# Half of the residual's transposition by a trip through HBM, and the stores of the squared tiles on GpSimd's queue

## The chip, the cores and the metric

The kernel runs on one core of a Trainium2 chip. The metric is device time of one execution in microseconds (us). Five engines work side by side, each in the order of its own program: PE (matrix products), DVE (VectorE), ACT (ScalarE), POOL (GpSimd) and SP. SP, ACT and POOL also issue DMA transfers.

## The reference

The reference computes one decoder layer on 256 tokens of width 2048 in fp32: two kinds of attention behind one input projection, an output projection, and a squared-ReLU MLP of width 8192. What this case touches is the line between attention and MLP:

```python
x   = x + RMSNorm_post(concat_heads(A, B) @ W_out)
x   = x + RMSNorm_post2(W_down relu(RMSNorm_pre2(x) @ W_up)^2)
```

## The kernel before

**Products.** Every fp32 operand is split into two rounded parts, hi by ACT (line 314, or 318 with a gain) and lo by DVE (line 315, or 319 with a gain). A block is the sum of three matrix products on PE: hi·hi, lo·hi and hi·lo, each 128x128 by 128x512, one every 0.227 us when nothing stalls (line 304).

**Stages.** Input projection, attention, output projection (accumulators acc_o), the residual with its norm, the up-projection (acc_u), its evacuation (ReLU and square), the down-projection (y), the last norm. b is one of the two halves of 128 tokens.

**The residual.** A generator `residual(b)` (949 to 983) makes x in four parts of 512 columns (line 958, DVE). Sixteen tiles of 128x128 of x are turned on PE (line 308, tile ht, four tiles to a group), each group is split to hT_hi (ACT) and hT_lo (DVE), the left operand of the up-projection. POOL stores x (xkeep, line 974); ACT squares x for the norm (junkx).

**The up-projection** has eight chunks j of 1024 columns. Chunk 0 takes sixteen k-steps (one per 128 rows of W_up), with a weight tile raw loaded by SP and split. Chunks 1 to 7 begin with k-steps 6 to 10, then alternate: step w0, k 11 and 12, w1, k 13, w2, k 14 and 15. A "w" step replaces two k-steps by seven products instead of eight (`seven`, 351 to 389). Its pair of weight tiles, 1 MB, is one load into one of two buffers, ab and ab2 (line 379, from POOL; (j,1) below means step w1 of chunk j). From that pair DVE makes sums, t (366) and u (370, 371), and ACT and DVE split the pair's part, u and t. Two w steps of chunk 6 and 7 (last one, last two) are loaded by SP tile by tile instead. The left operands' sums are made in `left_sums` (1137 to 1168).

**Evacuation.** After a chunk's last product DVE adds the seven products' part to the four accumulators (line 1259), then four emptyings follow, (b,n) = (0,0), (0,1), (1,0), (1,1): ACT does ReLU (1043) and square (1044) to a tile r, ACT's queue stores it (rkeep, 1046), and `turn_u` later loads it back in another layout (1059) and turns it on DVE (1061). The names rkeep2_1, r2_1 and so on are column block and b: chunk j has column blocks 2j and 2j+1.

**What sets the order.** The program order of each engine is written out by a small planner, `Flow`: a modelled clock and a list of generators with due times; each `yield x` puts the generator x us later on that clock, and `pump` runs those that are due between PE's products. Weight tiles are planned in one list; a w step's load (`fetch`) and its sums are emitted two tiles ahead of its first tile, at the same place. So the order in which POOL meets a load and a store is fixed here, while each engine runs as fast as its operands come:

```python
SUMS_AHEAD = 2
at = max(len(weights.specs) - SUMS_AHEAD, after)
for n, f in (*more, (0, fetch), (-late_sums, sums), *((0, f) for f in last)):
evac.append(flow.start(up_evac(2 * j + n, b, accs[b, n], o + 0.6)))
yield UP_STEP * order
```

Of the kernel before, what the change touches and what calls it, by code (L numbers as in the profile page):

```python
# [18 lines left out]
F32 = mybir.dt.float32  # L19
# [3 lines left out]
AF = mybir.ActivationFunctionType  # L23
# [15 lines left out]
FF = 4 * D  # L39
# [6 lines left out]
CW = 1024  # L46
# [45 lines left out]
D_PAIR, D_KR = 3.5, 6.0  # L92
D_LOADED, D_LATENT, D_KV = (13.0, 9.0), 3.0, (1.0, 5.0, 7.0)
D_X0, D_X, D_SS, D_TAB = 8.0, 3.0, 3.0, (14.0, 20.0)
D_NORM, D_HT, D_SECOND = 4.5, 1.5, 4.0

UP_STEP = 2.4

D_BACK, D_TURN, D_NEG, D_LO, D_ADD = 12.0, 8.0, 9.0, 2.0, 26.0

# [171 lines left out]
def layer(nc, tc, io):  # L272
# [652 lines left out]
    def powers():  # L925
# [18 lines left out]
        for b in range(NB):  # L944
            for c in (slice(0, CW), slice(CW, D)):
                nc.vector.tensor_scalar_mul(xs[b][:, c], xs[b][:, c], pw[:, b:b + 1])
                yield 1.5

    def residual(b):

        po, yg, hT = late["po"], late["yg"], late["hT"]
        nc.vector.reduce_sum(ssr[b][:, 0:1], ssy[b], axis=mybir.AxisListType.X)
        r = rstd_of(ssr[b][:, 0:1], 1, D, f"post{b}", (pws[:, 0, b:b + 1], pws[:, 1, b:b + 1]))

        def update(ns):
            cs = [slice(n * 512, (n + 1) * 512) for n in ns]
            for c in cs:
                nc.vector.scalar_tensor_tensor(out=xs[b][:, c], in0=yg[b][:, c], scalar=r, in1=xs[b][:, c],
                                               op0=OP.mult, op1=OP.add)

        update((0, 1))
        yield D_NORM
        for n in range(4):
            t = tp_bank(f"ht{n}{b}")
            for k in range(4):
                transpose(t[:, k * P:(k + 1) * P], xs[b][:, n * 512 + k * P:n * 512 + (k + 1) * P])
            tv = t.rearrange("p (k s) -> p k s", k=4)
            if n in (0, 1):
                update((n + 2,))
            split(hT[0][:, 4 * n:4 * n + 4, b * P:(b + 1) * P], hT[1][:, 4 * n:4 * n + 4, b * P:(b + 1) * P], tv)  # L970
            parts[b] += 1
            yield D_HT
        for q in range(4):
            nc.gpsimd.dma_start(out=xkeep[b][32 * q:32 * q + 32], in_=xs[b][q::4, :])
        for n in range(4):
            c = slice(n * 512, (n + 1) * 512)
            junk = po.tile([P, 512], BF16, tag="junk", bufs=1, name=f"junkx{n}{b}")
            nc.scalar.activation(junk, xs[b][:, c], AF.Square, accum_out=ssx[b][:, n:n + 1])
            yield 0.5
# [9 lines left out]
    def h_done(k, b):  # L989
        flow.until(lambda: 4 * parts[b] > k)  # L990

    res = [None] * NB
    for ns in ((0, 1), (2,), (3,)):
        if len(ns) == 2:
            order = [(c, t, b) for ts in (range(4), range(4, 6), range(6, 8)) for c in range(2) for t in ts for b in range(NB)]
        else:
            order = [(0, t, b) for t, b in in_order(8, (0, APART[0] if ns == (3,) else 0))]
        for c, b, acc in proj(mixT, [ch_o[n] for n in ns], f"o{ns[0]}", order, heads_done):
            n = ns[c]
            if not late:  # L1000
                flow.finish(*workers)
                pb.release()
                lat.release()
                hp = pool("hp", "left")
                late["hT"] = [hp.tile([P, KD, S], F32R, name=f"hT_{w}") for w in ("hi", "lo")]
                po = late["po"] = pool("po", "right")
                late["g_post"] = po.tile([P, D], F32, name="g_post")
                nc.sync.dma_start(out=late["g_post"],
                                  in_=io["norm_attn_post"].partition_broadcast(P).rearrange("p o d -> p (o d)"))
                late["yg"] = [po.tile([P, D], F32, name=f"yg{b}") for b in range(NB)]  # L1010
                for b_ in range(NB):
                    xs.append(po.tile([P, D], F32, name=f"x{b_}"))
                    nc.sync.dma_start(out=xs[b_], in_=io["x"][b_ * P:(b_ + 1) * P, :])
                pw_chain = flow.start(powers())
            out_evac(n, b, acc[0])
            if n == 3:
                flow.finish(pw_chain)
                weights.ahead = AHEAD_NORM
                res[b] = flow.start(residual(b), b * D_SECOND)
                flow.pump()  # L1020
    hT = late["hT"]

# [13 lines left out]
    def up_evac(j, b, acc, order):  # L1036
# [4 lines left out]
        else:  # L1041
# [1 line left out]
        nc.scalar.activation(r, acc, AF.Relu, scale=rstd2[b])  # L1043
        nc.scalar.activation(r, r, AF.Square)
        keep = dram.tile([P, 512], F32, name=f"rkeep{j}_{b}")
        nc.scalar.dma_start(out=keep.rearrange("(a t) (q c) -> (t q) a c", a=4, q=4),
                            in_=r.rearrange("m (a c) -> m a c", a=4))
        flow.start(turn_u(j, b, keep), D_BACK + (8.0 if (j, b) == (GT - 1, NB - 1) else 0.0))

# [87 lines left out]
    def left_sums(kp):  # L1137
# [4 lines left out]
        hs = [t[:, k:k + 2, :].rearrange("p k s -> p (k s)") for t in hT]  # L1142
        tt(out=f, in0=hs[0].bitcast(F32), in1=hs[1].bitcast(F32), op=OP.add)
        for i in range(2):
            nc.vector.tensor_scalar_mul(f[:, i * S:(i + 1) * S], f[:, i * S:(i + 1) * S], gcol[:, 8 + k + i:9 + k + i])
        fs, qs = [x.rearrange("p (k s) -> p k s", s=P) for x in (f, q)]
        keep = kp >= min(N_SEVEN[1:])
        n = 512 if keep else 384
# [51 lines left out]
    def closing():  # L1200
        return [late["c"][:, i * 512:(i + 1) * 512] for i in range(4)]

    PARTS = ((0, 0), (0, 1), (1, 0), (1, 1))
    evac = []
    for j in range(FF // CW):
# [4 lines left out]
        else:  # L1210
            accs = {bn: bank(i, f"acc_u{j}_{bn[0]}{bn[1]}") for bn, i in at.items()}
        steps = wide_u[j]
        order = in_order(len(steps), (APART[1], 0)) if j == 0 else [(t, b) for t, (w, _, _) in enumerate(steps)
                                                                    for b in range(NB if w == "k" else 1)]
        for t, b in order:
            what, k, tiles = steps[t]
            if (j, t, b) == (0, 8, 0):
                flow.finish(*res)
                late["po"].release()
                mix.release()  # L1220
                late["up"] = pool("up", "right")
# [34 lines left out]
        if j:  # L1256

            for bn in PARTS:
                nc.vector.tensor_tensor(out=accs[bn], in0=accs[bn], in1=more[bn], op=OP.add)
# [177 lines left out]
def arrays_of(inputs):  # L1437
# [3 lines left out]
    a["x"] = np.ascontiguousarray(a["x"][order])  # L1441
    a["xt"] = np.ascontiguousarray(np.concatenate([a["x"], inputs["norm_attn_pre"]]).T)
    a["pos"] = np.ascontiguousarray(inputs["positions"].reshape(S)[order].reshape(NB, P).T)
    a["gains"] = np.ascontiguousarray(np.concatenate(
        [inputs[n].reshape(-1, P) for n in ("q_latent_norm", "kv_latent_norm", "norm_mlp_pre")]).T)
    a["w_down"] = np.ascontiguousarray(
        a["w_down"].reshape(FF // 512, 4, 4, 32, D).transpose(0, 2, 1, 3, 4).reshape(FF, D))
    q = a["w_uq"].reshape(QR, HB, NOPE + RB)
    kv = a["w_ukv"].reshape(KVR, HB, NOPE + 128)
    a["w_uq"] = np.ascontiguousarray(np.concatenate([x.reshape(QR, -1) for x in (q[:, :, :NOPE], q[:, :, NOPE:])], axis=1))  # L1450
    a["w_ukv"] = np.ascontiguousarray(np.concatenate([x.reshape(KVR, -1) for x in (kv[:, :, :NOPE], kv[:, :, NOPE:])], axis=1))
    for n in ("norm_attn_post", "norm_mlp_post"):
        a[n] = np.ascontiguousarray(inputs[n])
    a["consts"] = shape_constants(order)
# [21 lines left out]
```

## Time and profile before

| what | us |
|---|---|
| median of the three runs shown (1020.38 to 1021.37) | 1020.69 |
| profiled execution | 1022.37 |
| its span, first to last instruction | 1020.6 |
| PE busy in the span | 1009.9 |
| DVE busy | 841.5 |
| ACT busy | 624.8 |
| POOL busy | 101.3 |

The profile page counts busy time per engine, cuts the span into 40 slices, follows back the chain of work that ended last, and groups instructions by line. All times of single instructions are counted from the span's start. A row of a timeline gives start, duration, engine, line, operation, tiles, and in brackets the idle time ahead of it with what ended it. A row of the windows table gives the window, then for PE, the weight loads, DVE, ACT and POOL the busy us and the count, the granted clock, the busy share of the DMA engines and GB/s.

### The profile page before, as it was taken

The page shows a single profiled execution, that of the slowest core. Times are in us where ns is not written, and L with a number is a line of the kernel's source. Part 1 is how long each engine was busy: PE and PEld are TensorE (multiplying, and loading weights), DVE is VectorE, ACT ScalarE, POOL GpSimd, SP SyncE. Part 2 cuts the span into 40 slices and gives each one's busy share as a digit, 9 for nine tenths or more (in the row PEclk, how much of TensorE's full clock was granted, in tenths as well). Part 3 has the DMA queues.
Part 4 walks back from the last instruction along what each step waited for, and adds up shares of the span by engine and source line. Part 5 has one row for each costly group of instructions (what it writes and reads, how often), then busy time and mean ns, then how long its engine had stood idle before and what let it go on. Part 6 is the DMA issues. An engine that isn't in the chain of part 4 may idle for free.

```text
span 1020.6 us, 13297 instructions
## 1 busy us (share of the span) xinstructions
PE 1009.9 (99%) x4670; PEld 842.0 (83%) x4670; DVE 841.5 (82%) x1127; ACT 624.8 (61%) x824; POOL 101.3 (10%) x160
## 2 busy tenths in 40 slices
PE   9999999999999999999999999999999999999996
PEld 6888889898888788888888888888878888888885
DVE  6676747676656779998999989897999999898985
ACT  6585446555463567676666775676666665767661
POOL 0020302102101200000010100000110000211100
PEclk9999999999999999999999999999999999999999
DMA  8977759656687478778988979679989867888952
GB/s 286 367 248 269 244 167 310 220 173 194 199 320 209 174 286 260 245 258 247 293 271 279 284 215 302 190 255 339 346 271 389 292 241 257 296 305 327 368 188 82
DMA packets 109170, 267.07 MB, mean 262 GB/s; under 512 B 9520, under 2 KB 28464, under 8 KB 108464
## 3 DMA queue, kind: packets, MB, share of 16 engines
q1 hardware_dynamic: 65584, 175.14, 50.2%
q0 software_dynamic: 20144, 71.31, 21.1%
q10 hardware_dynamic: 23376, 19.78, 6.2%
q8 instruction: 36, 0.59, 0.2%
q14 instruction: 30, 0.25, 0.1%
HBM read 232.64 MB, written 33.56 MB: 261 GB/s over the span
## 4 chain that ended last, share of the span: by engine, by line
PE 89%; DVE 5%; DMA 2%; issue 2%; ACT 1%; POOL 0%; ACTq 0%; DVEq 0%; POOLq 0%; SPq 0%
PE acc_u L304 26%; PE y L304 19%; PE acc_o L304 8%; PE m L304 6%; PE acc_v L304 5%; PE md L304 5%; PE acc_qk L304 4%; PE acc_q L304 3%; PE acc_k L304 3%; PE acc_ckv L304 3%; DVE lo L315 2%; PE acc_cq L304 2%; DMA rkeep<-uT 1%; PE sc_b L304 1%; DMA raw<-in_w_in 1%
## 5 line engine op out<-in xcount | busy, mean ns | idle before, releaser
L315 DVE TENSOR_TENSOR lo<-raw,hi 128x1024 fp32r<-128x1024 f32 (+2 forms) x205 | 233.4, 1157 | 66.6 <-ACT hi L314 65.4
L314 ACT ACTIVATE hi<-raw 128x1024 fp32r<-128x1024 f32 (+2 forms) x205 | 202.5, 1005 | 75.5 <-DMA raw<-in_w_in 22.8
L304 PE MATMUL acc_u<-hi,hT_lo 128*128 128x512 f32 x386 | 150.3, 389 | 0.5 <-DVE hT_lo L315 0.5
L304 PE MATMUL acc_u<-hi,hT_hi 128*128 128x512 f32 x386 | 150.7, 390 | 0.0
L304 PE MATMUL acc_u<-lo,hT_hi 128*128 128x512 f32 x386 | 150.2, 389 | 0.0
L304 PE MATMUL y<-lo,uhi 128*128 128x512 f32 x358 | 139.4, 389 | 0.4 <-DVE lo L315 0.4
L304 PE MATMUL y<-hi,ulo 128*128 128x512 f32 x358 | 139.4, 389 | 0.1
L304 PE MATMUL y<-hi,uhi 128*128 128x512 f32 x358 | 139.3, 389 | 0.0
L318 ACT ACTIVATE hi<-raw,gcol 128x1024 fp32r<-128x1024 f32 x86 | 96.7, 1148 | 34.2 <-DMA raw<-in_w_up 13.7
L319 DVE SCALAR_TENSOR_TENSOR lo<-raw,gcol,hi 128x1024 fp32r<-128x1024 f32 x86 | 106.6, 1274 | 9.7 <-ACT hi L318 9.6
L304 PEld LDWEIGHTS acc_u<-hi,hT_lo 128*128 128x128 f32 x386 | 72.4, 188 | 16.0 <-DVE hT_lo L315 0.9
L304 PEld LDWEIGHTS acc_u<-hi,hT_hi 128*128 128x128 f32 x386 | 72.5, 188 | 14.9
L304 PEld LDWEIGHTS acc_u<-lo,hT_hi 128*128 128x128 f32 x386 | 72.5, 188 | 14.8
L304 PEld LDWEIGHTS y<-lo,uhi 128*128 128x128 f32 x358 | 67.2, 188 | 14.7 <-DVE lo L315 0.8
L304 PEld LDWEIGHTS y<-hi,ulo 128*128 128x128 f32 x358 | 67.2, 188 | 14.4 <-DVE ulo L315 0.5
L304 PEld LDWEIGHTS y<-hi,uhi 128*128 128x128 f32 x358 | 67.2, 188 | 14.0
L315 DVE TENSOR_TENSOR lo<-st_down,hi 128x1024 fp32r<-128x1024 f32 x46 | 55.0, 1219 | 0.8 <-ACT hi L314 0.8
L304 PE MATMUL acc_o<-hi,mixT_hi 128*128 128x512 f32 x128 | 51.3, 401 | 0.0
L314 ACT ACTIVATE hi<-u 128x1024 fp32r<-128x1024 f32 (+1 forms) x33 | 32.3, 980 | 30.3 <-PE y L304 12.0
L304 PE MATMUL md<-hi,s 128*128 128x512 f32 x138 | 49.9, 389 | 0.0
L304 PE MATMUL acc_o<-hi,mixT_lo 128*128 128x512 f32 x128 | 49.9, 390 | 0.0
L304 PE MATMUL acc_o<-lo,mixT_hi 128*128 128x512 f32 x128 | 49.8, 389 | 0.0
(356 smaller groups left out, 2046.4 us busy)
## 6 DMA issues: line engine op xcount, KB each, us to landing
raw<-in_w_up SPq DMA_DIRECT2D x86, 512.0 KB, 4.9
raw<-in_w_down SPq DMA_DIRECT2D x82, 512.0 KB, 6.3
raw<-in_w_in SPq DMA_DIRECT2D x55, 512.0 KB, 5.6
ab<-in_w_up POOLq DMA_DIRECT2D x17, 1024.0 KB, 6.9
raw<-in_w_out SPq DMA_DIRECT2D x32, 512.0 KB, 4.6
ab_down<-in_w_down POOLq DMA_DIRECT2D x11, 1024.0 KB, 9.3
ulo<-ukeep POOLq DMA_DIRECT2D x20, 512.0 KB, 6.3
rkeep<-r ACTq DMA_DIRECT2D x28, 256.0 KB, 3.6
```

The source lines that it names most:

```text
L304: nc.tensor.matmul(out, a, b, start=start, stop=stop)
L314: nc.scalar.activation(hi, src, AF.Copy)
L315: nc.vector.tensor_tensor(out=lo, in0=src, in1=hi.bitcast(F32), op=OP.subtract)
L318: nc.scalar.activation(hi, src, AF.Copy, scale=g)
L319: nc.vector.scalar_tensor_tensor(out=lo, in0=src, scalar=g, in1=hi.bitcast(F32), op0=OP.mult, op1=OP.subtract)
```

## The change

Five things change.

1. Of each b, the upper half of x (columns 1024 to 2047) is no longer turned on PE. `trip` stores it to HBM (keeph, 512 KB, POOL), `turn_h` loads it back into yg (POOL), DVE turns it in two instructions of 128x512, and ACT and DVE split it from there. Sixteen of the 32 ht transposes go. Rows of W_up and their gains are permuted on the host to fit.
2. In chunk 0 the tiles of b=1 run two behind those of b=0 after the first seven tiles of both.
3. rkeep is stored from POOL's queue, not ACT's.
4. The third and fourth emptying of a chunk are due 1.9 and 1.4 us later on the planner's clock ((3.4 − 2.6) and (4.2 − 3.6), times UP_STEP 2.4).
5. In `left_sums` two multiplies by a gain move from DVE to ACT, and due times of the residual's steps are set anew.

On POOL, behind the residual, the queue of the kernel before holds the w steps' loads, one after the other (ab and ab2 are the two buffers, ukeep a store of transposed squares much later; rstd_pre2 is the norm's factor):

```order
L506 TENSOR_TENSOR rstd_pre21_3394<-t_pre21_3393,neg_half_85 128x1
L379 DMA ab2_3458<-in_w_up 128x2x1024
L379 DMA ab_3457<-in_w_up 128x2x1024
L379 DMA ab2_3458<-in_w_up 128x2x1024
L379 DMA ab_3457<-in_w_up 128x2x1024
L379 DMA ab2_3458<-in_w_up 128x2x1024
```

These are (1,1), (1,2), (2,0), (2,1) and (2,2); (1,0) is issued by SP. The same stretch with the change, to the load of (3,0):

```order
L507 TENSOR_TENSOR rstd_pre21_3468<-t_pre21_3467,neg_half_85 128x1
L1077 DMA rkeep0_0_3595<-r0_0_3592 128x4x128
L1077 DMA rkeep1_0_3614<-r1_0_3611 128x4x128
L1077 DMA rkeep0_1_3668<-r0_1_3665 128x4x128
L1077 DMA rkeep1_1_3691<-r1_1_3688 128x4x128
L380 DMA ab2_3478<-in_w_up 128x2x1024
L380 DMA ab_3477<-in_w_up 128x2x1024
L380 DMA ab2_3478<-in_w_up 128x2x1024
L1077 DMA rkeep2_0_4000<-r2_0_3997 128x4x128
L1077 DMA rkeep3_0_4023<-r3_0_4020 128x4x128
L1077 DMA rkeep2_1_4057<-r2_1_4054 128x4x128
L380 DMA ab_3477<-in_w_up 128x2x1024
```

The four stores of chunk 0 now stand ahead of (1,1), and of chunk 1's stores three stand ahead of (2,1); in each later chunk up to the sixth it is the same three. On ACT, at the end of chunk 1, before (u and t of step (2,0), hi166 is the hi part for k = 11 of chunk 2):

```order
L314 ACTIVATE hi164_4038<-u2_0_4013 128x1024
L1043 ACTIVATE r2_1_4051<-acc_u1_10_3645,rstd_pre21_3394 128x512
L1044 ACTIVATE r2_1_4051<-r2_1_4051 128x512
L1046 DMA rkeep2_1_4054<-r2_1_4051 128x4x128
L314 ACTIVATE hi165_4059<-t2_0_4012 128x1024
L1043 ACTIVATE r3_1_4072<-acc_u1_11_3646,rstd_pre21_3394 128x512
L1044 ACTIVATE r3_1_4072<-r3_1_4072 128x512
L1046 DMA rkeep3_1_4075<-r3_1_4072 128x4x128
L318 ACTIVATE hi166_4088<-raw166_4086,gcol_69 128x1024
```

and after:

```order
L315 ACTIVATE hi164_4028<-u2_0_4003 128x1024
L315 ACTIVATE hi165_4044<-t2_0_4002 128x1024
L1074 ACTIVATE r2_1_4054<-acc_u1_10_3633,rstd_pre21_3468 128x512
L1075 ACTIVATE r2_1_4054<-r2_1_4054 128x512
L319 ACTIVATE hi166_4073<-raw166_4071,gcol_69 128x1024
L1074 ACTIVATE r3_1_4080<-acc_u1_11_3634,rstd_pre21_3468 128x512
L1075 ACTIVATE r3_1_4080<-r3_1_4080 128x512
```

The third square, r2_1, moved behind the split of t, the fourth behind hi166, and the stores are gone from ACT. On DVE the same stretch, after, has the order that it had before:

```order
L316 TENSOR_TENSOR lo165_4045<-t2_0_4002,hi165_4044 128x1024
L367 TENSOR_TENSOR t2_1_4066<-ab_3477 128x1024
L371 TENSOR_TENSOR u2_1_4067<-t2_1_4066,ab_3477 128x512
L372 TENSOR_TENSOR u2_1_4067<-u2_1_4067,ab_3477 128x512
L320 SCALAR_TENSOR_TENSOR lo166_4074<-raw166_4071,gcol_69,hi166_4073 128x1024
```

The first reader of (2,1), t2_1, still follows lo165, the lo part of t2_0, directly. SP's queue is the same in both; on PE only the sixteen transposes are gone.

The diff, the host's part cut to its core:

```diff
--- before.py
+++ after.py
@@ -92,9 +92,10 @@
 D_PAIR, D_KR = 3.5, 6.0
 D_LOADED, D_LATENT, D_KV = (13.0, 9.0), 3.0, (1.0, 5.0, 7.0)
 D_X0, D_X, D_SS, D_TAB = 8.0, 3.0, 3.0, (14.0, 20.0)
-D_NORM, D_HT, D_SECOND = 4.5, 1.5, 4.0
-
-UP_STEP = 2.4
+D_NORM, D_HT, D_SECOND = (4.5, 4.8), (1.5, 2.5), 2.5
+D_AWAY, D_HERE, D_GROUP, D_SQUARE, D_KEEP = (9.0, 3.0), (6.8, 8.0), (1.2, 0.1), (4.0, 5.5, 8.5), 3.5
+UP_STEP, EVAC = 2.4, (0.6, 1.6, 3.4, 4.2)
 
 D_BACK, D_TURN, D_NEG, D_LO, D_ADD = 12.0, 8.0, 9.0, 2.0, 26.0
 
@@ -946,6 +947,22 @@
                 nc.vector.tensor_scalar_mul(xs[b][:, c], xs[b][:, c], pw[:, b:b + 1])
                 yield 1.5
 
+    def turn_h(b, keep):
+        back, turned = [late["yg"][b][:, i * CW:(i + 1) * CW] for i in range(2)]
+        nc.gpsimd.dma_start(out=back.rearrange("p (n f) -> p n f", n=2), in_=keep.rearrange("(n p) f -> p n f", p=P))
+        yield D_HERE[b]
+        hT = late["hT"]
+        tv = [turned[:, i * 512:(i + 1) * 512].rearrange("p (k s) -> p k s", k=4) for i in range(2)]
+        for i in range(2):
+            nc.vector.transpose(tv[i].rearrange("p k (t q) -> p k q t", q=4),
+                                back[:, i * 512:(i + 1) * 512].rearrange("p (q k c) -> p k q c", q=4, k=4))
+            yield D_GROUP[b]
+        for i in range(2):
+            split(*[x[:, 8 + 4 * i:12 + 4 * i, b * P:(b + 1) * P] for x in hT], tv[i])
+            parts[b] += 1
+            yield 0.3
     def residual(b):
 
         po, yg, hT = late["po"], late["yg"], late["hT"]
@@ -958,25 +975,39 @@
                 nc.vector.scalar_tensor_tensor(out=xs[b][:, c], in0=yg[b][:, c], scalar=r, in1=xs[b][:, c],
                                                op0=OP.mult, op1=OP.add)
 
+        def trip():
+            update((2, 3))
+            keep = dram.tile([2 * P, 512], F32, name=f"keeph{b}")
+            nc.gpsimd.dma_start(out=keep.rearrange("(g t) (q c) -> (t q) g c", g=8, q=4),
+                                in_=xs[b][:, CW:].rearrange("m (g c) -> m g c", g=8))
+            res.append(flow.start(turn_h(b, keep), D_AWAY[b]))
         update((0, 1))
-        yield D_NORM
-        for n in range(4):
+        if not b:
+            trip()
+        yield D_NORM[b]
+        for n in range(2):
             t = tp_bank(f"ht{n}{b}")
             for k in range(4):
                 transpose(t[:, k * P:(k + 1) * P], xs[b][:, n * 512 + k * P:n * 512 + (k + 1) * P])
             tv = t.rearrange("p (k s) -> p k s", k=4)
-            if n in (0, 1):
-                update((n + 2,))
             split(hT[0][:, 4 * n:4 * n + 4, b * P:(b + 1) * P], hT[1][:, 4 * n:4 * n + 4, b * P:(b + 1) * P], tv)
             parts[b] += 1
-            yield D_HT
+            if b and not n:
+                trip()
+            yield D_HT[b]
+        if b:
+            yield D_KEEP
         for q in range(4):
             nc.gpsimd.dma_start(out=xkeep[b][32 * q:32 * q + 32], in_=xs[b][q::4, :])
+        yield D_SQUARE[2 * b]
         for n in range(4):
             c = slice(n * 512, (n + 1) * 512)
             junk = po.tile([P, 512], BF16, tag="junk", bufs=1, name=f"junkx{n}{b}")
             nc.scalar.activation(junk, xs[b][:, c], AF.Square, accum_out=ssx[b][:, n:n + 1])
             yield 0.5
+        if not b:
+            yield D_SQUARE[1]
         nc.vector.reduce_sum(ssr[b][:, 1:2], ssx[b], axis=mybir.AxisListType.X)
         rstd2[b] = rstd_of(ssr[b][:, 1:2], 1, D, f"pre2{b}", (1.0 / D, pws[:, 2, b:b + 1]))
         if b == NB - 1:
@@ -989,7 +1020,7 @@
     def h_done(k, b):
         flow.until(lambda: 4 * parts[b] > k)
 
-    res = [None] * NB
+    main, res = [None] * NB, []
     for ns in ((0, 1), (2,), (3,)):
         if len(ns) == 2:
             order = [(c, t, b) for ts in (range(4), range(4, 6), range(6, 8)) for c in range(2) for t in ts for b in range(NB)]
@@ -1016,7 +1047,7 @@
             if n == 3:
                 flow.finish(pw_chain)
                 weights.ahead = AHEAD_NORM
-                res[b] = flow.start(residual(b), b * D_SECOND)
+                main[b] = flow.start(residual(b), b * D_SECOND)
                 flow.pump()
     hT = late["hT"]
 
@@ -1043,7 +1074,7 @@
         nc.scalar.activation(r, acc, AF.Relu, scale=rstd2[b])
         nc.scalar.activation(r, r, AF.Square)
         keep = dram.tile([P, 512], F32, name=f"rkeep{j}_{b}")
-        nc.scalar.dma_start(out=keep.rearrange("(a t) (q c) -> (t q) a c", a=4, q=4),
+        nc.gpsimd.dma_start(out=keep.rearrange("(a t) (q c) -> (t q) a c", a=4, q=4),
                             in_=r.rearrange("m (a c) -> m a c", a=4))
         flow.start(turn_u(j, b, keep), D_BACK + (8.0 if (j, b) == (GT - 1, NB - 1) else 0.0))
 
@@ -1142,7 +1173,8 @@
         hs = [t[:, k:k + 2, :].rearrange("p k s -> p (k s)") for t in hT]
         tt(out=f, in0=hs[0].bitcast(F32), in1=hs[1].bitcast(F32), op=OP.add)
         for i in range(2):
-            nc.vector.tensor_scalar_mul(f[:, i * S:(i + 1) * S], f[:, i * S:(i + 1) * S], gcol[:, 8 + k + i:9 + k + i])
+            nc.scalar.activation(f[:, i * S:(i + 1) * S], f[:, i * S:(i + 1) * S], AF.Copy, scale=gcol[:, 8 + k + i:9 + k + i])
+        yield 1.0
         fs, qs = [x.rearrange("p (k s) -> p k s", s=P) for x in (f, q)]
         keep = kp >= min(N_SEVEN[1:])
         n = 512 if keep else 384
@@ -1164,7 +1196,7 @@
     def all_sums():
         for kp in range(2):
             yield from left_sums(kp)
-        yield 8.0
+        yield 1.0
         yield from left_sums(2)
 
     def three(out, a, w, first, last):
@@ -1200,6 +1232,12 @@
     def closing():
         return [late["c"][:, i * 512:(i + 1) * 512] for i in range(4)]
 
+    def up_order(n):
+        f, lag = APART[1], 2
+        pairs = [x for t in range(f, n) for x in ((t, 0), (t - lag, 1)) if x[1] == 0 or x[0] >= f]
+        return ([(t, b) for b in range(NB) for t in range(f)] + pairs + [(t, 1) for t in range(n - lag, n)])
     PARTS = ((0, 0), (0, 1), (1, 0), (1, 1))
     evac = []
     for j in range(FF // CW):
@@ -1210,12 +1248,12 @@
         else:
             accs = {bn: bank(i, f"acc_u{j}_{bn[0]}{bn[1]}") for bn, i in at.items()}
         steps = wide_u[j]
-        order = in_order(len(steps), (APART[1], 0)) if j == 0 else [(t, b) for t, (w, _, _) in enumerate(steps)
+        order = up_order(len(steps)) if j == 0 else [(t, b) for t, (w, _, _) in enumerate(steps)
                                                                     for b in range(NB if w == "k" else 1)]
         for t, b in order:
             what, k, tiles = steps[t]
-            if (j, t, b) == (0, 8, 0):
-                flow.finish(*res)
+            if (j, t, b) == (0, 11, 0):
+                flow.finish(*main, *res)
                 late["po"].release()
                 mix.release()
                 late["up"] = pool("up", "right")
@@ -1258,7 +1296,7 @@
             for bn in PARTS:
                 nc.vector.tensor_tensor(out=accs[bn], in0=accs[bn], in1=more[bn], op=OP.add)
             for o, (b, n) in enumerate(PARTS):
-                evac.append(flow.start(up_evac(2 * j + n, b, accs[b, n], o + 0.6)))
+                evac.append(flow.start(up_evac(2 * j + n, b, accs[b, n], EVAC[o])))
     weights.ahead = W_AHEAD
     u_last = evac[-4:]
     up = late["up"]
@@ -1441,14 +1479,18 @@
...
+    half = a["w_up"].reshape(4, 4, 4, 32, FF)
+    a["w_up"] = np.concatenate([half[:2], half[2:].transpose(0, 2, 1, 3, 4)]).reshape(D, FF)
...
```

More of the change, by code (lines that the diff above doesn't have):

```diff
@@ L1443, in arrays_of @@
     a["pos"] = np.ascontiguousarray(inputs["positions"].reshape(S)[order].reshape(NB, P).T)
-    a["gains"] = np.ascontiguousarray(np.concatenate(
-        [inputs[n].reshape(-1, P) for n in ("q_latent_norm", "kv_latent_norm", "norm_mlp_pre")]).T)
     a["w_down"] = np.ascontiguousarray(
@@ L1451, in arrays_of @@
     a["w_ukv"] = np.ascontiguousarray(np.concatenate([x.reshape(KVR, -1) for x in (kv[:, :, :NOPE], kv[:, :, NOPE:])], axis=1))
+    half = a["w_up"].reshape(4, 4, 4, 32, FF)
+    a["w_up"] = np.concatenate([half[:2], half[2:].transpose(0, 2, 1, 3, 4)]).reshape(D, FF)
+    half = inputs["norm_mlp_pre"].reshape(4, 4, 4, 32)
+    pre = np.concatenate([half[:2], half[2:].transpose(0, 2, 1, 3)])
+    a["gains"] = np.ascontiguousarray(np.concatenate(
+        [g.reshape(-1, P) for g in (inputs["q_latent_norm"], inputs["kv_latent_norm"], pre)]).T)
     for n in ("norm_attn_post", "norm_mlp_post"):
```

## The prediction

> **What bounds the kernel now.** I read the page's busy table first, then its chain, then the waits of PE and of POOL.
>
> ```profile
> PE 1009.9 (99%) x4670; PEld 842.0 (83%) x4670; DVE 841.5 (82%) x1127; ACT 624.8 (61%) x824; POOL 101.3 (10%) x160
> PE 89%; DVE 5%; DMA 2%; issue 2%; ACT 1%; POOL 0%; ACTq 0%; DVEq 0%; POOLq 0%; SPq 0%
> PE acc_u L304 <- DVE hT_lo L315: 0.5, 1, 0.5
> PE y L304 <- DVE lo L315: 0.4, 1, 0.4
> POOL ab L379 <- DVE lo L315: 216.4, 16, 29.8
> ```
>
> PE is the bound, and hardly waits: from the MLP's start on, 0.5 us for hT_lo and 0.4 for a lo part. The third waits row is the one that matters here: POOL stood at the w steps' loads for 216 us in all, at most 29.8 at once, until a buffer came free. It waits in place, at the head of its queue, and that costs nothing today because nothing urgent stands behind. How near the next engine is to being a bound shows in the windows of one chunk each (the second, and the seventh, whose last two pairs come by SP):
>
> ```profile
> 428.50:470.00 41.50, 41.50 (x185) 34.37 (x184) 39.08 (x44) 28.05 (x32) 2.14 (x3) 1.00 0.78 254
> 635.90:677.40 41.50, 41.50 (x185) 34.37 (x184) 37.05 (x44) 26.40 (x31) 0.00 (x0) 1.00 0.68 218
> ```
>
> A chunk takes PE 41.5 us, and DVE works 39.08 of them. DVE can lose 2.4 us a chunk, and what it loses beyond that PE must wait for.
>
> **The transposes that go.** One group of four, between its neighbours:
>
> ```profile
> 339.74 0.40 PE L304 MATMUL acc_o<-hi,mixT_lo 128*128 128x512 f32 x1
> 339.97 0.60 PE L308 MATMUL ht<-ident,x 128*128 128x128 f32 x4
> 340.33 0.48 PE L304 MATMUL acc_o<-hi,mixT_hi 128*128 128x512 f32 x1
> 340.64 0.40 PE L304 MATMUL acc_o<-lo,mixT_hi 128*128 128x512 f32 x1
> 340.88 0.40 PE L304 MATMUL acc_o<-hi,mixT_lo 128*128 128x512 f32 x1
> 341.11 0.39 PE L304 MATMUL acc_u<-hi,hT_hi 128*128 128x512 f32 x1
> ```
>
> From 339.97 to 341.11 are 1.14 us for the group and three products; three at 0.227 (340.88 to 341.11 is 0.23) are 0.68, so a group costs 0.46, and four groups 1.84. The stall of 0.5 for hT_lo, with the slower start behind it 0.74, may go with them: at best 2.6 us less on PE. What comes in their place (a 512-KB store, a load, two DVE turns and two splits for each b) runs beside products; for b=1 there is little time, and at worst it takes back the 2.6. But none of this reaches the end if PE then waits in chunk 1, and it does, by the following.
>
> **The loads that now stand behind stores.** The order rows ahead show it: each load (j,1), j = 1 to 6, sits on POOL behind the third square's store of the chunk before (for j = 1, behind the fourth of chunk 0). When were these loads issued before?
>
> ```profile
> 363.64 0.76 POOL L379 DMA_DIRECT2D ab<-in_w_up  x1 [0.42 <-ACT hi L318]
> ...
> 413.69 0.71 POOL L379 DMA_DIRECT2D ab<-in_w_up  x1 [8.26 <-DVE lo L315]
> 435.64 0.71 POOL L379 DMA_DIRECT2D ab<-in_w_up  x1 [21.23 <-DVE lo L315]
> ...
> 477.22 0.71 POOL L379 DMA_DIRECT2D ab<-in_w_up  x1 [22.34 <-DVE lo L315]
> 477.93 0.97 POOL L1087 DMA_DIRECT2D ukeep<-uT  x1
> ```
>
> The first row is (1,1), the second (2,1), the third (2,2): as soon as a buffer was free. The last two show a store that stands behind a load and leaves only behind it. Their readers, on DVE, and the squares on ACT:
>
> ```profile
> 397.16 1.22 DVE L366 TENSOR_TENSOR t<-ab 128x1024 f32<-128x1024 f32 x1
> ...
> 428.54 2.48 DVE L1259 TENSOR_TENSOR acc_u<-acc_u,c 128x512 f32<-128x512 f32 x4
> 438.13 1.23 DVE L315 TENSOR_TENSOR lo<-t,hi 128x1024 fp32r<-128x1024 f32 x1 [1.52 <-ACT hi L314]
> 439.28 1.22 DVE L366 TENSOR_TENSOR t<-ab 128x1024 f32<-128x1024 f32 x1
> 441.87 1.28 DVE L319 SCALAR_TENSOR_TENSOR lo<-raw,gcol,hi 128x1024 fp32r<-128x1024 f32 x1
> ...
> 396.49 0.63 ACT L1044 ACTIVATE r<-r 128x512 f32<-128x512 f32 x1
> 435.96 0.63 ACT L1044 ACTIVATE r<-r 128x512 f32<-128x512 f32 x1
> 436.63 0.37 ACTq L1046 DMA_DIRECT2D rkeep<-r  x1
> 437.04 1.06 ACT L314 ACTIVATE hi<-t 128x1024 fp32r<-128x1024 f32 x1 [0.44 <-ACT r L1044]
> ```
>
> Before, (2,1) had 25.6 us from issue (413.69) to first use (439.28), and (1,1) 33.5. After, (2,1) can be issued only when the third square is made and its store issued, and that square (435.96 to 436.59 here) goes behind the split of t (437.04). Without the store's place on ACT the split starts about 0.4 earlier and another 1.3 earlier without relu and square ahead of it, at 435.3 (behind hi<-u, which ends at 435.36); split 1.06, relu and square 1.3: the square ends some 9.0 us behind the start of the addition at 428.54, at 437.6. Prices for the rest, from two tiles' rows (the second gives min, median, max from issue to landing of ab):
>
> ```profile
> L701 POOL DMA_DIRECT2D keepq<-q x4: 752/764/942, 68.2 to 102.2; - x4
> DMA to landing us min/median/max: 5.2/7.1/11.3
> ```
>
> POOL needs 0.76 for a store of rkeep's kind (keepq is the nearest), then the load lands 5.2 to 7.1 us on. I take 6.1, halfway: the stalled kernel loads less beside it, which speaks for the minimum, and the store just ahead in the queue speaks for the median. So the load lands at 428.54 + 9.0 + 0.76 + 6.1 = 444.4, where DVE, whose lo<-t moves up by about 1.5 with ACT's split, asks for it at about 437.6: a wait of 6.8 in the middle of its chunk. DVE is in order: behind the waiting t stand both u, lo for k = 11, and all weights after them.
>
> The Trainium skill, "DMA: Bandwidth & Descriptors", section "Anatomy of one DMA", fits a POOL-issued transfer as 2.0 us plus bytes at 436 GB/s; for 1 MiB this is an estimate of 4.4 us, and no load of ab landed in under 5.2 here. By it the sum below would be six times 1.7, or 10 us, smaller; the trace's bounds are used.
>
> **What a chunk then takes.** From t to the next chunk's addition DVE has hardly a gap:
>
> ```profile
> 439.27:470.12 30.85, 30.85 (x137) 25.53 (x136) 30.08 (x33) 19.99 (x22) 1.43 (x2) 1.00 0.82 276
> 481.53:511.85 30.32, 30.32 (x136) 25.10 (x135) 29.97 (x33) 20.09 (x22) 2.34 (x3) 1.00 0.94 289
> ```
>
> 30.08 and 29.97 of work; I take 30.3 us. The period is 9.0 + 0.76 + 6.1 + 30.3 = 46.2 us against 41.5: 4.7 more a chunk.
>
> Chunk 1 first. Its load (1,1) waits for chunk 0's fourth square, which ended at 397.12. In the change ACT also makes the gains' multiplies there, and DVE hands work to it and back; I put the square at 400 (bounds 397 and 402). Issue and landing: 400 + 0.76 + 6.1 = 406.9, against 397.16 when t read it. With 30.9 to the next addition it comes at 437.8, 9.2 late. Five more chunks (2 to 6) add 4.7 each: the addition behind chunk 6 is 32.7 late. Chunk 7 has no such load on POOL.
>
> PE is less late than DVE, since DVE was ahead. Its lo for k = 11 was done at 443.15, and by the chain the products came at
>
> ```profile
> 446.94 1.36 PE m L304 x6
> 448.30 5.44 PE acc_u L304 x24
> ```
>
> 5.2 us later. PE uses that lead up first and ends chunk 6 about 27.5 late. In chunk 7 DVE has 4.4 us of room (37.05 of 41.5), enough to get most of the lead back; for the down-projection, where DVE is nearly as full, I add 0.8, half a us being PE's only such wait there today. Sum: +28.3.
>
> **The other edits.** The ACT queue loses 32 issues (0.37 us a piece), worth nothing where PE and DVE set the pace. The later due times are the reason why the squares stand behind the split, counted above. The order of b1's tiles and the gain's multiplies on ACT shift work of engines that have room in chunk 0; nothing beyond the bounds of the last square.
>
> The span becomes 1020.6 + 28.3 = 1048.9; the profiled execution was 1.77 longer than its span (1022.37), and 1.68 above the median of 1020.69. So the forecast is 1049.0 us.
>
> **Rivals.**
>
> *Faster: the queue does not hold the loads* (chance 0.07). If a load reached the head of POOL 7 us ahead of its reader after all, since the stores leave earlier than I read from the order, DVE never waits and only PE's savings stay: 1020.69 − 1.84 − 0.74 = about 1018. For it: POOL is busy 10%. Against: the third square cannot precede its accumulator's addition (428.54 at the earliest), 11 us ahead of t, and the order puts the split between. The Trainium skill bears on it, same page, section "Issuing engines are not separate DMA queues": issuing from several engines saves only the sequencer's time to issue. By that alone the stores' move would be worth nothing; the same page says that a semaphore wait is spent on the issuing sequencer, which the row of 216.4 us agrees with.
>
> *No change* (0.02): savings and a shorter wait cancel.
>
> *Only the first wait counts* (0.04): from chunk 2 on the squares come early enough, and just (1,1) is late. Then lo for k = 11 of chunk 1, at 399.75 + 1.28 = 401.0 before, is done 9.7 us later, at 410.8, and PE loses that less a lead of 5.2 as in chunk 2, so 4.5; less the saving of 1.84: about 1023. Against: the order rows are alike in each chunk.
>
> *Slower still* (0.05): a load behind its own queue's store lands like the down-projection's:
>
> ```profile
> ab_down<-in_w_down POOLq DMA_DIRECT2D x11, 1024.0 KB, 9.3
> ```
>
> 9.3 instead of 6.1, six times 3.2: about 1067.
>
> **How the numbers follow.** The forecast's own case has 0.82, all slower. Landing between 5.2 and 7.1 moves it by −5.4 to +6, chunk 0's last square by −3 to +2, the residual by up to −2.6, and a lead that is not regained before the down-projection by up to 5: its own range is 1041 to 1056. The asked range, with tails of all these at once, is 1036 to 1062; it leaves out the two near or below the old time and the one near 1023 (0.13 together) and part of the 1067. About 0.2%, 2 us, is what a measurement can tell from no change: faster 0.07, within it 0.02, slower 0.82 + 0.04 + 0.05 = 0.91.
>
> **What would show it.** In the changed kernel's profile: DVE's t of each (j,1) idle for 5 to 8 us with the DMA of ab as releaser, six times, and no such wait at (j,0) and (j,2); POOL's ab issued within a us of a store of rkeep; chunk windows of about 46 us with PE waiting 4 to 5 us for lo at k = 11; chunk 7 back at 41.5. The residual's part would be PE's products of chunk 0 closing 1.8 to 2.6 us earlier, and the gain lost in chunk 1. I am wrong if POOL's ab rows come 20 us ahead of their t, or if DVE's waits there are under 3 us: then DVE's room covers them.

## The result and the profile after

The changed kernel takes 1056.4 us (1055.4 to 1057.6 in five runs), the kernel before 1020.6; the ratio is 1.0351, interval 1.0336 to 1.0366. The forecast was 1049, with 1036 to 1062 around it. The profiled execution has a span of 1055.8 us against 1020.6. Its busy table and chain:

```profile
PE 1018.0 (96%) x4654; PEld 846.6 (80%) x4654; DVE 843.8 (80%) x1125; ACT 624.2 (59%) x830; POOL 129.0 (12%) x196
PE 39%; issue 11%; DVE 6%; DMA 4%; ACT 2%; POOL 1%; DVEq 0%; POOLq 0%; ACTq 0%
```

The engines have hardly more to do. PE has 16 records fewer (the transposes); it is 37.8 us idle in place of 10.7, and its busy time is 8 us longer all the same (the last section shows where), and the chain that was PE for 89% now is PE for 39%. The waits of PE, DVE and POOL say where the rest is:

```profile
PE acc_u L305 <- DVE lo L320: 26.8, 6, 7.3
DVE t L367 <- DMA ab<-in_w_up: 44.5, 6, 8.2
POOL rkeep L1077 <- ACT r L1075: 183.5, 27, 24.9
```

Six times DVE waits for a load of ab, 44.5 us in all, and six times PE waits for the lo part behind it. POOL, which stood 216.4 us at loads of ab until a buffer was free, now stands 183.5 us at stores until a square is made, and 67.2 us at these loads. POOL's timeline at the end of chunk 1, and DVE's:

```profile
443.47 0.76 POOL L1077 DMA_DIRECT2D rkeep<-r  x1 [1.40 <-ACT r L1075]
448.20 0.75 POOL L1077 DMA_DIRECT2D rkeep<-r  x1 [3.97 <-ACT r L1075]
448.94 0.71 POOL L380 DMA_DIRECT2D ab<-in_w_up  x1
450.48 0.78 POOL L1077 DMA_DIRECT2D rkeep<-r  x1 [0.83 <-ACT r L1075]
```

```profile
438.90 2.49 DVE L1297 TENSOR_TENSOR acc_u<-acc_u,c 128x512 f32<-128x512 f32 x4
446.90 1.22 DVE L316 TENSOR_TENSOR lo<-t,hi 128x1024 fp32r<-128x1024 f32 x1
455.74 1.23 DVE L367 TENSOR_TENSOR t<-ab 128x1024 f32<-128x1024 f32 x1 [7.62 <-DMA ab<-in_w_up]
...
486.06 2.49 DVE L1297 TENSOR_TENSOR acc_u<-acc_u,c 128x512 f32<-128x512 f32 x4
```

The load of (2,1), issued at 413.69 before, is issued at 448.94, directly behind the third store; its data come at 455.7, and DVE, which asked at 448.1, stands for 7.6 us. From one addition to the next are 47.16 us instead of 41.5.

### The profile page after: what moved, and what is told of

Read it like the earlier page. It is cut to its first block, busy times and chain, and to the rows that moved or that the text cites. A ratio compares the mean times of both kernels' runs of the same rounds, so it can differ in the third digit from the quotient of the medians.

```text
span 1055.8 us, 13302 instructions
## 1 busy us (share of the span) xinstructions
PE 1018.0 (96%) x4654; PEld 846.6 (80%) x4654; DVE 843.8 (80%) x1125; ACT 624.2 (59%) x830; POOL 129.0 (12%) x196
## 4 chain that ended last, share of the span: by engine, by line
PE 39%; issue 11%; DVE 6%; DMA 4%; ACT 2%; POOL 1%; DVEq 0%; POOLq 0%; ACTq 0%
PE y L305 25%; PE acc_u L305 7%; PE md L305 6%; DMA ab<-in_w_up 4%; DVE lo L320 2%; PE m L305 2%; DVE lo L316 1%; DVE t L367 1%; POOL rkeep L1077 1%; ACT hi L315 1%; DVE u L371 1%; PE y L1382 1%; ACT r L1074 0%; DMA ukeep<-neg 0%; ACT hi L319 0%
## 5 line engine op out<-in xcount | busy, mean ns | idle before, releaser
L305 PE MATMUL acc_u<-lo,hT_hi 128*128 128x512 f32 x386 | 155.1, 402 | 26.8 <-DVE lo L320 26.8
L305 PE MATMUL acc_u<-hi,hT_lo 128*128 128x512 f32 x386 | 153.9, 399 | 0.0
L305 PE MATMUL acc_u<-hi,hT_hi 128*128 128x512 f32 x386 | 153.9, 399 | 0.0
L305 PEld LDWEIGHTS acc_u<-lo,hT_hi 128*128 128x128 f32 x386 | 74.8, 194 | 45.0 <-DVE lo L320 29.3
L305 PEld LDWEIGHTS acc_u<-hi,hT_lo 128*128 128x128 f32 x386 | 74.9, 194 | 15.7
L305 PEld LDWEIGHTS acc_u<-hi,hT_hi 128*128 128x128 f32 x386 | 74.7, 193 | 16.0
L305 PEld LDWEIGHTS y<-lo,uhi 128*128 128x128 f32 x358 | 67.2, 188 | 14.0
L305 PEld LDWEIGHTS y<-hi,ulo 128*128 128x128 f32 x358 | 67.2, 188 | 14.0
L305 PEld LDWEIGHTS y<-hi,uhi 128*128 128x128 f32 x358 | 67.2, 188 | 13.8
L367 DVE TENSOR_TENSOR t<-ab 128x1024 f32<-128x1024 f32 x18 | 22.0, 1221 | 44.5 <-DMA ab<-in_w_up 44.5
L315 ACT ACTIVATE hi<-u 128x1024 fp32r<-128x1024 f32 (+1 forms) x33 | 32.3, 979 | 37.4 <-DVE u L372 17.5
L315 ACT ACTIVATE hi<-ab 128x512 fp32r<-128x512 f32 (+1 forms) x36 | 29.4, 835 | 36.2 <-DMA ab<-in_w_up 26.7
```

The lines of the kernel that those rows point to most:

```text
L305: nc.tensor.matmul(out, a, b, start=start, stop=stop)
L315: nc.scalar.activation(hi, src, AF.Copy)
L367: tt(out=two[0], in0=two[1][:, 0:2, :], in1=two[1][:, 1:4:2, :], op=OP.add)
```

## The experiments

The theory: the loads (j,1) stand behind the stores on POOL, and DVE, in order too, waits for them. The rivals: the trip of h costs the time; the later emptyings do; stores issued by POOL are slow or contend with the loads wherever they stand.

**Undo the queue alone.**

```diff
-        nc.gpsimd.dma_start(out=keep.rearrange(...
+        nc.scalar.dma_start(out=keep.rearrange(...
```

> The changed kernel with one thing undone: the squared tiles are stored from ACT's queue again. The trip of h, the order of b1's tiles and the later emptyings stay. Theory (the w steps' loads stand behind the stores on POOL and DVE waits for them): the waits of t for ab go from 44.5 us to under 1, and only PE's savings stay, 1016 to 1020 us. Rival 1 (the trip of h, its DVE turns and its waits cost): it stays above 1030. Rival 2 (the later squares cost, because the accumulators come free later): it stays above 1030 too, and PE waits for ACT's r before m.

Measured 1020.0 us, ratio 0.9997 (0.9988 to 1.0006). No wait of t for ab is left, and the 35 us are gone: without the queue's edit the other four make no slowdown. The runs lie between 1018.3 and 1022.3, more scatter than the kernel before shows beside them (1020.2 to 1021.2), so the median is at the upper edge of what was expected; the profiled execution itself was 1018.3.

**The queue alone, in the kernel before,** and the queue with the later emptyings:

```diff
-        nc.scalar.dma_start(out=keep.rearrange(...
+        nc.gpsimd.dma_start(out=keep.rearrange(...
```

> The kernel before with one thing done: the squared tiles are stored from POOL's queue. No trip, emptyings due as before. On POOL each load (j,1) then stands behind the fourth store of the chunk before, whose square comes at about the same time as the third square of the changed kernel, since both squares keep their early place on ACT. Theory: t of each (j,1) waits 6 to 8 us for ab, period 46 to 48 us, 1048 to 1060 us, the whole slowdown with none of the other edits. Rival (the slowdown needs the later emptyings, or the trip's extra transfers): under 1035.

> The kernel before with the stores on POOL and the later emptyings, without the trip. With stores on POOL alone it was 1054.2 us. Theory: the load stands behind the third store, whose square comes behind the split of t, so the wait is that of the changed kernel, 7 to 8 us, and the time is 1052 to 1058 us. Rival (the later emptyings ease the wait, since only three stores stand ahead): under 1045.

Measured 1054.2 us (1.0320, 1.0306 to 1.0334) and 1053.5 (1.0325, 1.0310 to 1.0341). The waits of DVE in the first of the two, and one period:

```profile
DVE t L366 <- DMA ab<-in_w_up: 43.2, 6, 8.4
480.57 2.49 DVE L1259 TENSOR_TENSOR acc_u<-acc_u,c 128x512 f32<-128x512 f32 x4
497.82 1.22 DVE L366 TENSOR_TENSOR t<-ab 128x1024 f32<-128x1024 f32 x1 [6.98 <-DMA ab<-in_w_up]
528.14 2.49 DVE L1259 TENSOR_TENSOR acc_u<-acc_u,c 128x512 f32<-128x512 f32 x4
```

A change of one word in the kernel before costs 33 us: the trip and the later emptyings are not needed for it. Behind four early stores (emptyings as before) or three later ones t starts at about the same time, 17.5 and 17.3 us behind the addition on average. So the queue's edit is enough by itself for 33 of the 36 us; where the last 3 come from these runs do not show.

**Keep the stores on POOL, move the loads ahead of them.**

```diff
-        for n, f in (*more, (0, fetch), (-late_sums, sums), ...
+        for n, f in (*more, (early, fetch), (-late_sums, sums), ...
...
+ early=4 if k == 1 else 0
```

> The changed kernel with the stores left on POOL, but each load (j,1) emitted four tiles earlier, so that on POOL it stands ahead of the four stores of the chunk (for j = 1 behind the first two stores of chunk 0). Same transfers, same queues, only the place in POOL's queue differs. Theory: the waits of t go to near 0 and the time to 1016 to 1021 us, as with the stores on ACT. Rival (stores issued by POOL are slow or contend with the loads wherever they stand): waits of 3 us or more a chunk stay, 1035 or more.

Measured 1027.5 us (1.0064, 1.0049 to 1.0079). Twenty-nine of the 36 us are gone with the same transfers on the same queue, so for these it is the place in the queue that costs. The full recovery that was expected did not come, and DVE's timeline says why:

```profile
482.18 1.22 DVE L367 TENSOR_TENSOR t<-ab 128x1024 f32<-128x1024 f32 x1
496.02 1.22 DVE L367 TENSOR_TENSOR t<-ab 128x1024 f32<-128x1024 f32 x1 [4.77 <-DMA ab<-in_w_up]
```

t of (3,1), at 482.18, no longer waits. The next one, (3,2), does. Its load's place on POOL:

```profile
484.63 0.75 POOL L1077 DMA_DIRECT2D rkeep<-r  x1 [1.53 <-ACT r L1075]
485.37 0.71 POOL L380 DMA_DIRECT2D ab<-in_w_up  x1
```

It stands behind the fourth store, next in line. The wait has moved one load on and become smaller (14.3 us in four instead of 44.5 in six). That this load takes 10.6 us to land, where those of (j,1) took 6 to 7 in the changed kernel, the place alone does not explain. While it was under way (485.4 to 496.0) the DMA engines were 95% busy and moved 333 GB/s, against 86% and 273 GB/s for the load of (2,1) in the changed kernel (449.0 to 455.7); among the transfers beside it were the next load of ab, issued at 489.27, and stores. Which of them slows it was not tried, so a part of the rival stands for these 7 us.

**The first wait by itself**: the same edit for j = 2 to 6 only.

```diff
+ early=4 if k == 1 and j > 1 else 0
```

> The changed kernel with the loads (j,1) of j = 2 to 6 emitted four tiles earlier, ahead of the stores, and (1,1) left behind chunk 0's four stores. Beside the version with all of them earlier (1027.5 us) this prices the one wait at (1,1). Theory (one wait of 8 us costs its length less DVE's lead, and DVE regains nothing while its later waits stay): t of (1,1) waits about 8 us, PE stalls 6 to 8 us once at k = 11 of chunk 1, 1031 to 1036 us. Rival (the first wait is absorbed by DVE's room in the chunks behind): 1027 to 1029.

Measured 1035.6 us (1.0145, 1.0131 to 1.0159). t of (1,1) waits 7.96 us and PE 6.9 at k = 11 of chunk 1. Against the version above, which differs in this one load, the wait at (1,1) costs 8.1 us, give or take some 2 by the two intervals: about its whole length, where the theory took DVE's lead off. So DVE gets little or nothing of it back later, which fits its waits at (j,2) in the chunks behind (16.3 us here, 14.3 there).

**A dose**: the same edit, with the load one place further ahead than in the changed kernel, behind the second store.

```diff
+ early=1 if k == 1 else 0
```

> A dose: each load (j,1) emitted one tile earlier, so that it stands on POOL behind the second store of the chunk before instead of the third (for j = 1 behind the third of chunk 0 instead of the fourth). Theory: in the changed kernel the second store was issued by 444.2, 4.7 us ahead of the third's load; the wait of t falls from 7.4 to about 2.8 us a chunk, 0.4 over DVE's room of 2.4, so the period goes from 47.2 to about 42.5 us: with chunk 1's own wait of 3.5, 1022 to 1032 us. Rival (place in the queue is not what counts): 1050 or more. Rival (any store ahead stops the queue for as long): above 1045.

Measured 1028.9 us (1.0080, 1.0056 to 1.0103), inside the expected range. Waits, and the additions behind chunk 1 and chunk 5:

```profile
DVE t L367 <- DMA ab<-in_w_up: 13.5, 6, 3.0
435.09 2.49 DVE L1297 TENSOR_TENSOR acc_u<-acc_u,c 128x512 f32<-128x512 f32 x4
...
604.08 2.49 DVE L1297 TENSOR_TENSOR acc_u<-acc_u,c 128x512 f32<-128x512 f32 x4
```

The wait falls from 7.4 us to 2.3 on average, and the period to 42.2 (169.0 us for four), 0.7 over PE's 41.5. Of five us less of wait all five come back; of the last 2.3 DVE's room covers two thirds.

**The other parts alone.** The trip, the order of b1's tiles and the gains on ACT, with stores and emptyings as in the kernel before (against the changed kernel):

```diff
-UP_STEP, EVAC = 2.4, (0.6, 1.6, 3.4, 4.2)
+UP_STEP, EVAC = 2.4, (0.6, 1.6, 2.6, 3.6)
...
-        nc.gpsimd.dma_start(out=keep.rearrange(...
+        nc.scalar.dma_start(out=keep.rearrange(...
```

> The kernel before with the trip of h, the new order of b1's tiles and the gain's multiplies on ACT alone; stores on ACT's queue and emptyings due as before. Theory: nothing of the slowdown is here; PE saves 1.84 us of transposes and perhaps the 0.74 of one stall, so 1017.5 to 1019.5 us. Rival (the trip is late for b1 and PE waits for hT_lo): 1020.5 to 1025.

The later emptyings alone, in the kernel before:

```diff
-                evac.append(flow.start(up_evac(2 * j + n, b, accs[b, n], o + 0.6)))
+                evac.append(flow.start(up_evac(2 * j + n, b, accs[b, n], EVAC[o])))
```

> The kernel before with the later emptyings alone: third and fourth square behind the split of t on ACT, stores on ACT's queue. Theory: the split of t comes earlier, DVE loses its idle 1.5 us ahead of lo<-t in each chunk and gains on PE; PE is the bound, so at most its 0.5 to 1 us of stalls in the down-projection goes: 1019.3 to 1020.9 us. Rival (the later emptyings keep accumulators from PE): above 1022 with PE waiting for ACT's r.

The trip alone: 1023.6 us (1.0033, 1.0018 to 1.0048), slower where a gain of 2 to 3 us was expected, though PE did not wait for hT_lo. Its profile has PE waiting for lo parts instead, 0.7 us in chunk 1 and 2.5 in chunk 7. DVE idles ahead of lo<-t, and it enters the chunks late:

```profile
PE acc_u L305 <- DVE lo L320: 3.2, 2, 2.5
400.24 1.22 DVE L367 TENSOR_TENSOR t<-ab 128x1024 f32<-128x1024 f32 x1
430.54 2.49 DVE L1297 TENSOR_TENSOR acc_u<-acc_u,c 128x512 f32<-128x512 f32 x4
648.68 1.23 DVE L316 TENSOR_TENSOR lo<-t,hi 128x1024 fp32r<-128x1024 f32 x1 [1.52 <-ACT hi L315]
```

PE starts the chunks earlier by what it saved; DVE comes 3.1 us later to t of (1,1) (397.16 before) and 2.0 later to the addition behind chunk 1 (428.54 before). With these idle times its chunk takes 41.7 us (from 513.31 to 555.02 between two additions), more than PE's 41.5, so that a smaller lead runs out. This shows why the saving is lost; it does not show why the run is slower, for the profiled execution, at 1022.2 us, is the fastest of the seven (up to 1028.4) and level with the profiled one of the kernel before (1022.4). The idle time ahead of lo<-t was there before too (1.52 us at 438.13). The later emptyings take it away: with them (the first run above) the additions of chunk 1 and 2 are 40.1 us apart, at 429.50 and 469.62, and the next three periods are 40.6 to 40.8:

```profile
429.50 2.49 DVE L1297 TENSOR_TENSOR acc_u<-acc_u,c 128x512 f32<-128x512 f32 x4
469.62 2.49 DVE L1297 TENSOR_TENSOR acc_u<-acc_u,c 128x512 f32<-128x512 f32 x4
```

Alone they are worth nothing, 1021.1 us (1.0001, 0.9992 to 1.0009), since there PE is the bound. So edits 1 and 4 belong together.

**A version without the queue's cost.** Two numbers on top of the first run: b1 four tiles behind, and b1's turn later.

```diff
-    f, lag = APART[1], 2
+    f, lag = APART[1], 4
-D_AWAY, D_HERE, ... = (9.0, 3.0), (6.8, 8.0), ...
+D_AWAY, D_HERE, ... = (9.0, 3.0), (6.8, 10.7), ...
```

> The changed kernel with its stores back on ACT, and two numbers more: b1's tiles run four behind b0's in chunk 0 instead of two, and b1's turn on DVE is due 2.7 us later. In the profiles so far DVE stood 1.7 to 4.9 us in place at b1's turn, until yg<-keeph had landed, and once PE then waited 1.2 us for hT_lo. Theory (that wait is what makes the runs with the trip scatter over 4 us): the wait falls under 1 us, and the time to 1017.5 to 1018.8 us with less scatter, under both kernels. Rival (the scatter has another source): 1019.5 to 1021, as with two behind.

> The changed kernel with its stores back on ACT, once more, beside the version with the later turn on the same chip. Theory: 1019 to 1021 us with scatter; in its profile DVE's idle time at b1's turn goes with the time.

Measured on one chip: 1019.9 (0.9993, 0.9984 to 1.0002) with the later turn, 1019.5 (0.9985, 0.9976 to 0.9994) without. The wait at the turn, 3.9 us in the profile without, is gone with it, and the time is the same: this theory of the scatter fell. What both profiles share is a stall of PE at k = 11 of chunk 1, 1.1 and 1.7 us, for lo:

```profile
399.93 1.23 DVE L316 TENSOR_TENSOR lo<-t,hi 128x1024 fp32r<-128x1024 f32 x1 [1.04 <-ACT hi L315]
401.07 1.22 DVE L367 TENSOR_TENSOR t<-ab 128x1024 f32<-128x1024 f32 x1
```

(the later turn's DVE): t of (1,1) at 401.1, which came at 397.2 in the kernel before, while PE is earlier. Edit 5, the gains on ACT, and the sums' later beginning are the suspects, since DVE waits for ACT there. Taking these back:

```diff
-            nc.scalar.activation(f[:, i * S:(i + 1) * S], ..., AF.Copy, scale=gcol[...])
-        yield 1.0
+            nc.vector.tensor_scalar_mul(f[:, i * S:(i + 1) * S], ..., gcol[...])
...
-            if (j, t, b) == (0, 11, 0):
+            if (j, t, b) == (0, 10, 0):
```

> The changed kernel with stores on ACT, b1's tiles four behind and its turn later, and the left operands' sums as in the kernel before: gains on DVE again, and begun one tile earlier (at k = 10 of chunk 0). In the profile of the later turn the one stall left on PE was 1.3 us for lo of k = 11 in chunk 1, where DVE had idled between the sums' steps, and its t came at 401.1 against 397.2 in the kernel before. Theory (the scatter and the missing gain are DVE's lateness at the head of chunk 1): that stall goes and the time is 1017.3 to 1018.8 us. Rival (something before chunk 0 scatters): 1019 to 1021 as before.

Measured 1018.6 us, ratio 0.9979 (0.9970 to 0.9988), with t of (1,1) back in its old place and no stall of PE from chunk 0 on:

```profile
397.39 1.22 DVE L367 TENSOR_TENSOR t<-ab 128x1024 f32<-128x1024 f32 x1
```

The trip together with the later emptyings is worth 0.2%, faster than both kernels. How much of it comes from taking edit 5 back the times do not settle: this run was on another chip than the two ahead of it, and its interval touches theirs (0.9984 to 1.0002 with the later turn, 0.9976 to 0.9994 without). The scatter stays (1017.8 to 1021.0), so it has a source that these runs do not show.

## Why the prediction was right, step by step

*POOL's queue holds the loads.* Right. It was read from the order of the instructions with one row of waits in the profile; the runs that change nothing but the queue, or nothing but the place in it, show it from both sides.

*The place and number of the waits.* Right: t of (j,1), j = 1 to 6, and no other.

*The terms of a period*, over chunks 2 to 6 of the profile after: from the addition to the load's issue 9.76 was forecast; it was 10.0 in chunk 2 (438.90 to 448.94) and 10.4 to 10.8 in the others, mean 10.5. From issue to t, 6.1 was taken between 5.2 and 7.1; it was 6.2 to 6.8, mean 6.4. From t to the next addition, 30.3 was forecast and it was 30.3 in each. Together 47.2 instead of 46.2. The way to the load's issue was mis-sized by 0.75 and the landing by 0.3, five times over: these are 5 of the 7 us by which the sum was short. The first has two parts, on ACT in chunk 2 and chunk 3:

```profile
447.28 0.63 ACT L1075 ACTIVATE r<-r 128x512 f32<-128x512 f32 x1
491.97 0.64 ACT L1106 ACTIVATE neg<-uT 128x512 fp32r<-128x512 f32 x1 [1.63 <-DMA ukeep<-neg]
```

In chunk 2 the third square ended 9.0 behind the addition (447.91), as forecast, but its store began only 0.29 later, at 448.20, and such a step the sum did not have. In chunks 3 to 6 the square ended 9.4 to 9.8 behind the addition, because ACT also makes neg there, ahead of the split of u (in chunk 3 u was ready at 491.73 and its split began at 492.51); chunk 2, whose rows the forecast was read from, has none. The rows that show the last of the period, the additions behind chunk 6 and 7:

```profile
675.14 2.48 DVE L1297 TENSOR_TENSOR acc_u<-acc_u,c 128x512 f32<-128x512 f32 x4
716.81 2.48 DVE L1297 TENSOR_TENSOR acc_u<-acc_u,c 128x512 f32<-128x512 f32 x4
```

675.1 against the forecast 668.8, and chunk 7, without a store ahead of its loads, 41.7 long where 41.5 was forecast.

*Chunk 1.* The last square's store was issued at 399.62 (forecast 400), but its load took 8.2 us and not 6.1:

```profile
399.62 0.75 POOL L1077 DMA_DIRECT2D rkeep<-r  x1 [2.37 <-ACT r L1075]
400.37 1.43 POOL L380 DMA_DIRECT2D ab<-in_w_up  x2
```

The x2 is what I had not costed: (1,2) stood in the queue right behind (1,1), its buffer long free, and 2 MB went out at once. But this does not explain the 8.2 by itself. With the stores on POOL in the kernel before, (2,1) and (2,2) go out as such a pair too, and the first was there in 6.0:

```profile
444.31 1.42 POOL L379 DMA_DIRECT2D ab<-in_w_up  x2
450.26 1.22 DVE L366 TENSOR_TENSOR t<-ab 128x1024 f32<-128x1024 f32 x1 [6.96 <-DMA ab<-in_w_up]
```

What else slowed it is open. The addition came at 438.9, 1.1 later than forecast.

*PE's lead.* 5.2 less 0.8, 4.4 in all, was forecast to be taken off DVE's lateness behind chunk 6. The rows of the kernel before:

```profile
614.28 0.39 PE L304 MATMUL acc_u<-lo,hT_hi 128*128 128x512 f32 x1
637.04 2.48 DVE L1259 TENSOR_TENSOR acc_u<-acc_u,c 128x512 f32<-128x512 f32 x4
```

and of the changed one, with the window behind its last stall:

```profile
648.80 0.50 PE L305 MATMUL acc_u<-lo,hT_hi 128*128 128x512 f32 x1 [4.07 <-DVE lo L320]
648.80:652.80 4.00, 4.00 (x11) 3.17 (x12) 4.00 (x5) 2.41 (x3) 0.82 (x2) 0.57 0.95 319
```

The addition behind chunk 6 is 38.1 late (675.14 against 637.04) and the span 35.2 longer, so 2.9 came off, not 4.4, and by other steps. The forecast set the old addition at 636.04, by PE's period of 41.5; DVE's additions were 41.6 to 41.8 apart before, so its lateness is 1.0 less than that. For the same reason its lead over PE had shrunk: lo for k = 11 of chunk 6 was done at 610.65 and used at 614.28, a lead of 3.6, not the 5.2 of chunk 2. PE's product of it comes 34.5 late. Then the slow clock behind the stall (the last section) costs 1.8, a term that the forecast did not have: at the first m product of step w1 PE is 36.3 late (655.77 against 619.50). From there on PE waits no more. In the down-projection, where the forecast added 0.8, 1.0 comes back, because PE is held up there in the kernel before (at 742 and 753 us, the second time by a stall of 0.36) and not in the changed one. That 2.9 lies near 4.4 is in part luck: of the forecast's two terms one was too large and the other had the wrong sign, and a third was missing. With the 5 us of the periods and the 1.1 of chunk 1, less 1.0 for the old addition's place, the 1.5 too little here make up the 7.

*The residual.* From the first transposed group to the first product of step w0 of chunk 1 on m (338.14 to 401.90 before, 338.94 to 400.03 after) PE was 2.67 us faster; 1.84 + 0.74 was forecast. It was lost in chunk 1, as forecast. That it would be a gain once the queue is put right, as the rival of 1018 us implied, is not clear for the stores alone: put back on ACT they gave 0.9997 in one series and 0.9985 in another. A gain of 0.2% was measured only for the version that also changed b1's tiles and turn and gave DVE its time back.

Two slips in the sums, neither of which bears on the forecast: six times 3.2 on top of 1049 makes the rival of the slower landing 1068, not 1067, and 439.28 less 1.5 is 437.8, not 437.6.

## What to carry to other kernels

A queue that issues transfers is an engine in program order: before a store is moved to it, look at which load stands behind the store, and when the store's operand is made. Idle share says nothing of that: POOL was busy 10% of the time before and 12% after, and held up the kernel by 3.5%. And a saving on the bound engine counts only as far as the next engine is ahead of it; here two edits that were worth nothing or less by themselves (later emptyings, the trip) made a gain of 0.2% together, with a third one taken back and a fourth (the order of b1's tiles) changed.

## What the runs showed that was not expected

After a stall PE came back slow. In the changed kernel, chunk 3, a PE timeline and three windows, of chunks 3, 2 and 4 (the granted clock is the third number from the end):

```profile
506.92 0.80 PE L305 MATMUL acc_u<-lo,hT_hi 128*128 128x512 f32 x1 [5.43 <-DVE lo L320]
507.51 0.63 PE L305 MATMUL acc_u<-hi,hT_lo 128*128 128x512 f32 x1
507.94 0.63 PE L305 MATMUL acc_u<-hi,hT_hi 128*128 128x512 f32 x1
507.00:511.00 4.00, 4.00 (x10) 3.13 (x11) 4.00 (x5) 2.33 (x3) 0.91 (x2) 0.50 0.88 291
459.40:463.40 4.00, 3.73 (x16) 3.08 (x17) 4.00 (x5) 3.55 (x5) 0.56 (x1) 1.00 0.86 276
554.20:558.20 4.00, 4.00 (x12) 3.20 (x13) 4.00 (x5) 2.39 (x3) 0.84 (x2) 0.63 0.91 296
```

For four us behind the stall of 5.4 the clock was 0.50 and a product took 0.43 us instead of 0.227; behind the stall of 3.2 us in chunk 2 it stayed 1.00. The Trainium skill, "TensorE: Matmul & The Clock Gate", part 1, tells of a half clock after an idle window of about 3.4 us that runs free of the program, until a busy window is over. The longer stalls of the changed kernel agree with it: 7.3 and 5.4 us (0.50), 4.1 and 4.0 us (0.57). Shorter ones do not: in chunk 4 products 3.16 us apart from start to start (551.03 and 554.19, 2.8 us of it idle) were enough for the half clock during part of the four us (0.63), and so was a stall of 2.1 us in the run that leaves only (1,1) late (597.26, clock 0.65). So the length of a stall alone does not tell, and the measurement differs from the page there.

Up to the last stall this did not set the time, for DVE took the same 30.3 us from t to the addition in each chunk, and PE's slower products only fill time that it would have stood at the next stall. Behind the last one, in chunk 6, PE has no wait left that could take it up, and the 1.8 us are in the total, as the part on PE's lead shows.
